# The opening of a stream encoder: five early v blocks of one column piece, a written order on every engine, x in the tiles' own rooms

## The chip, the cores and the metric

The kernel runs on one core of a Trainium2 chip. The metric is the device time of one execution in microseconds. Three runs of the kernel before took 2201.74 to 2204.34 us, median 2202.23.

## The reference

One step of a two-layer encoder for 1024 prompt frames and 32 sample frames, 1024 channels, in float32. Layer 0 mixes by a gated MLP, layer 1 by pooling; each is followed by a feed-forward part. Only the beginning of layer 0 matters here:

```python
mod = jax.nn.silu(c) @ w_ada[i] + b_ada[i]
sh1, sc1, gt1, sh2, sc2, gt2 = jnp.split(mod[:, None, :], N_MOD, axis=-1)
h = rmsnorm(x, g_norm[i, 0]) * (1 + sc1) + sh1
...
z = jax.nn.gelu(h @ w_in)
u, v = jnp.split(z, 2, axis=-1)
v = rmsnorm(v, g_v)
```

The condition c goes through SiLU and a matrix of 6144 columns to shifts and scales; x is normalised, scaled and shifted to h; the right half of h @ w_in is v, 2048 columns wide. All of v is needed before its norm, and so before the gating, can go on.

## The kernel before, in words

**Tiles.** The frames stand in three tiles of 384, 384 and 256 + 32 columns, with channels on the partitions: `acc[t]` holds x transposed. x comes in nine blocks of 128 frames (the ninth has the 32 sample frames); `do_x` squares a block on ACT for the sum of squares and transposes it with eight matmuls (line 548), and DVE copies the two halves into `acc` (line 551).

**Split products.** Every operand of a large product is split in two float32r parts: hh and hl for h, wh and wl for a weight. `do_w` makes wh on ACT (line 392) and wl on DVE (a helper at line 79) from a raw load of 512 KB. A product of a block with eight 128-row slices of a weight piece then takes 24 matmuls, three per slice (lines 876 to 878): wh with hh, wl with hh, wh with hl. `v_mm` issues them, `v_end` applies the GELU, sums squares and stores the result to `vd` (line 890).

**v in pieces and blocks.** v has four column pieces p of 512, and nine blocks b of frames (blocks 0 to 2 are tile 0, 3 to 5 tile 1, 6 to 8 tile 2). A piece's weight comes in four items q, two channel slices each.

**The ada slices.** Shifts and scales come in slices of 256 columns, each from two loads. The first eight slices (0 to 3 shift, 4 to 7 scale) are multiplied on TensorE (`do_ada_pe`, line 424: four matmuls per load, which the trace shows as eight); ACT copies the result (adas, line 436), two matmuls transpose it (adat, line 441), DVE reduces it (adar, line 443) and writes `mod` and `coef`. Later slices are summed on DVE (aa).

**The norm of a tile.** `first_norm(t)` is a generator. Its first part is `spread`: DVE makes the factor per frame (ms_h, r_h), ACT writes it on diagonals (line 684), TensorE broadcasts them (pb_h, line 686) and ACT copies the result (line 840). Then `apply` goes through the eight channel slices: mt on DVE (x times coef times factor), hh on ACT (plus shift, rounded, line 823), hl on DVE (the rest). Each `next` advances it by a slice.

**The opening.** Five blocks get PSUM banks at once: (0,0), (0,1), (0,2), (1,0), (1,1), as (piece, block), all of tile 0. In round q (0 to 3) the ada slices 4+q and q, the items q of both pieces, and two slices of tile 0's norm are made, then the five blocks take their products with item q, 30 matmuls. In between, round 2 takes x blocks 3 to 5 and tile 1's statistics, round 3 blocks 6 to 8 and tile 2's. After the rounds come the rest of the norms, the ends of the five blocks, and then the other blocks in `v_order`, first (1,2), then blocks 3 to 8 of pieces 0 and 1, then pieces 2 and 3.

**Loads.** `stream` is the list of loads in the order in which they are made into operands; `issue` puts them on SP's queue ahead of use. x, the v items and later loads take one of three raw buffers; the early ada loads take slots of the weight pool (16). The row vectors (conditions, norm gains, biases) are loaded from ACT's queue at the very beginning.

**Order.** The instructions are recorded in the order of the program, and a scheduler may move them within an engine. `time["dve"]` and `time["pe"]` are the planner's own clocks, which decide when later stream items are taken in; they measure nothing.

Of the kernel before, what the change touches and what calls it, by code (L numbers as in the profile page):

```python
# [15 lines left out]
P = 128  # L16
D = 1024
# [17 lines left out]
def tile_stream_encoder_step(  # L35
# [119 lines left out]
    def t_raw(name):  # L155
        return work.tile([P, 1024], F32, tag="raw", bufs=RAW_SLOTS, name=name)
# [9 lines left out]
            (sgu_g_v.rearrange("o (k p) -> (o k) p", p=P), 16),  # L166
        ],
    ]
    vecs = []
    for i, parts in enumerate(rows):  # L170
        n = sum(k for _, k in parts)
        raw = t_m(f"row{i}")
        at = 0
        for ap, k in parts:
            nc.scalar.dma_start(raw[at : at + k, :P], ap)
            at += k
        if i == 2:
            act(out=raw[0:16, P : 2 * P], in_=raw[0:16, :P], func=AF.Silu)
        pt = ps_ms(f"rowT{i}")
        nc.tensor.transpose(pt[:, :n], raw[:n, :P], ident[:n, :n])  # L180
        if i == 2:
            nc.tensor.transpose(pt[:, 64:80], raw[0:16, P : 2 * P], ident[0:16, 0:16])
        v = const.tile([P, n], F32, name=f"vec{i}")
        nc.vector.tensor_copy(v, pt[:, :n])
        vecs.append(v)
        if i == 2:
            csil = const.tile([P, KB, NV], F32, name="csil")
            nc.vector.tensor_copy(csil, pt[:, 64:80].rearrange("p (v k) -> p k v", v=NV))
            csil32 = work.tile([P, NV, 256], F32, tag="aa", bufs=2, name="csil32").rearrange(
                "p v (k m) -> p (v k) m", m=32  # L190
            )[:, 0:KB, :]
            nc.vector.memset(csil32, 0.0)
            nc.vector.tensor_copy(csil32[:, :, 0:NV], csil)
    gT = vecs[0]
    bT = vecs[1]
    pscale = vecs[2][:, 16:24]
# [127 lines left out]
    for b in range(3):  # L324
        add_x(b)
    for q in range(4):
        if q == 3:
            for b in range(3, 6):
                add_x(b)
        for j in (8 + 2 * q, 9 + 2 * q, 2 * q, 2 * q + 1):  # L330
            add_ada(0, j)
        for p in range(2):
            add_w(*v_item(p, q))
    first_ada = len(stream)
    for b in range(6, 9):
# [28 lines left out]
    deferred = []  # L364

    def in_raw(k):
        return not (stream[k][0] == "ada" and k < first_ada)
# [439 lines left out]
    def apply(t, l, cf, sh, r, keep=False):  # L807
        hh[t] = room("h", t, f"hh{l}_{cf}_{t}", F32R)
        hl[t] = room("l", t, f"hl{l}_{cf}_{t}", F32R)
        for k in range(KB):  # L810
            for c0, w, v in segs[t]:
                x = A(t, k, c0, w)
                a = t_m(f"mt{t}_{k}_{v}")[:, :w] if keep else x
                stt(
                    out=a,
                    in0=x,
                    scalar=coef[:, l, cf, v, k : k + 1],
                    in1=r[:, c0 : c0 + w],
                    op0=ALU.mult,
                    op1=ALU.mult,  # L820
                )
                b = mod[:, l, sh * 8 + k, v : v + 1]
                act(out=hh[t][:, k, c0 : c0 + w], in_=a, func=AF.Identity, bias=b, scale=1.0)
                stt(
                    out=hl[t][:, k, c0 : c0 + w],
                    in0=a,
                    scalar=b,
                    in1=hh[t][:, k, c0 : c0 + w].bitcast(F32),
                    op0=ALU.add,
                    op1=ALU.subtract,  # L830
                )
            yield False
# [24 lines left out]
    def v_mm(ps, p, b, ks):  # L857
        if b < 8:
            t, c0, m = min(b // 3, 2), (b - 3 * min(b // 3, 2)) * P, P
        else:  # L860
            t, c0, m = 2, 256, DEC
        for k in ks:
            wh, wl = need_w(("v", p, k // 2))
            o = (k % 2) * 512
            if b == 8:
                a = hs[k // 4][:, k % 4, :]
                tick(0.46)
                mm(ps[: 2 * m, :], a, wh[:, o : o + 512], start=k == 0, stop=False)
# [7 lines left out]
            mm(ps[:m, :], a_h, wh[:, o : o + 512], start=k == 0, stop=False)  # L876
            mm(ps[:m, :], a_h, wl[:, o : o + 512], start=False, stop=False)  # L877
            mm(ps[:m, :], a_l, wh[:, o : o + 512], start=False, stop=k == KB - 1)  # L878
# [25 lines left out]
    early_ps = [(ps_dn if i < 3 else ps_up)(f"pv{p}_{b}") for i, (p, b) in enumerate(early)]  # L904
    h0, h1, h2 = (first_norm(t) for t in range(NT))
    stream_to("x", 2)
    statistics(h0)
    stream_to("ada", (0, 0, 1))
    for q in range(4):
        stream_to("w", ("v", 0, q))  # L910
        next(h0)
        stream_to("w", ("v", 1, q))
        next(h0)
        if q < 2:
            stream_to("ada", (0, q + 1, 1))
        elif q == 2:
            stream_to("x", 5)
            statistics(h1)
            stream_to("ada", (0, 3, 1))
        else:  # L920
            stream_to("x", 8)
            statistics(h2)
        for ps, (p, b) in zip(early_ps, early):
            v_mm(ps, p, b, (2 * q, 2 * q + 1))
    for h in (h0, h1):
        for _ in h:
            pass
    for ps, (p, b) in zip(early_ps, early):
        v_end(ps, p, b)
    for _ in h2:  # L930
        pass

    hs = []
    for half in range(2):
# [619 lines left out]
```

## Time and profile before

| what | value |
|---|---|
| median of three runs | 2202.23 us |
| the profiled execution's own time | 2204.23 us |
| its span, first to last instruction | 2202.4 us |
| mean granted TensorE clock | 0.998 |
| early x blocks | 9 loads, 512 KB each but the last |
| loads of the first four rounds (x blocks 6 to 8 with them) | 33 |

The profile has a page of totals and views of the trace. A row of the timeline gives start and duration in us, engine, line, operation, what is written and read, shapes, how many instructions are merged (x16), and in brackets how long the engine had been idle and what ended that. PE is TensorE; PEld is its weight load, which runs beside it; ACT is ScalarE, DVE is VectorE, SP issues most loads; a q behind an engine's name means the issue of transfers. A window row gives start and end, length, and for each engine its busy us and number of instructions, then the granted TensorE clock, the busy share of the DMA engines, and GB/s.

### The profile page before, as it was taken

How to read it: one execution, taken by the hardware profiler on the slowest of the kernel's cores; microseconds unless marked ns; L12 is line 12 of the kernel's file. 1: busy time of each engine (PE TensorE's matmuls, PEld its weight loads, DVE VectorE, ACT ScalarE, POOL GpSimd, SP SyncE). 2: the span in 40 equal slices, each digit the busy share in tenths (PEclk: the TensorE clock that was granted, in tenths of full speed). 3: DMA queues.
4: the chain of work that ended last, by engine and by line, in shares of the span. 5: the costliest groups of instructions: out<-in, count | busy, mean ns of one | idle time of the engine just before them, and what ended most of it. 6: DMA issues, size and time to landing. Idle time of an engine off the chain costs nothing.

```text
span 2202.4 us, 33445 instructions
## 1 busy us (share of the span) xinstructions
PE 2179.8 (99%) x13383; PEld 2095.2 (95%) x13383; DVE 1378.1 (63%) x2439; ACT 986.7 (45%) x1675; POOL 0.7 (0%) x6
## 2 busy tenths in 40 slices
PE   7999999999999999999999999999999999999998
PEld 4777899999999999999999999999999999999998
DVE  4945746566869546575747879879775554523375
ACT  4633422134447552323445566656564542313354
POOL 0000000000000000000000000000000000000000
PEclk9999999999999999999999999999999999999999
DMA  8565624343527443344645465655454552302343
GB/s 278 181 210 166 198 87 131 89 144 117 154 82 220 148 147 122 101 133 122 191 126 153 149 179 177 183 184 158 142 171 143 154 153 64 109 10 77 97 121 111
DMA packets 354753, 312.98 MB, mean 142 GB/s; under 512 B 10819, under 2 KB 316427, under 8 KB 354597
## 3 DMA queue, kind: packets, MB, share of 16 engines
q1 hardware_dynamic: 352596, 309.95, 46.2%
q8 instruction: 105, 1.72, 0.3%
q10 hardware_dynamic: 2000, 0.89, 0.2%
q14 instruction: 52, 0.42, 0.1%
HBM read 278.95 MB, written 31.84 MB: 141 GB/s over the span
## 4 chain that ended last, share of the span: by engine, by line
PE 97%; DMA 1%; ACT 1%; DVE 1%; issue 0%; SPq 0%; DVEq 0%; ACTq 0%
PE pf L849 11%; PE pf L850 11%; PE pf L851 11%; PE pg L849 11%; PE pg L850 11%; PE pg L851 11%; PE pu L849 3%; PE pu L851 3%; PE pu L850 3%; PE po L849 3%; PE po L850 3%; PE po L851 3%; PE pv L876 3%; PE pv L877 2%; PE pv L878 2%; PE psp L1096 1%
## 5 line engine op out<-in xcount | busy, mean ns | idle before, releaser
L849 PE MATMUL pg<-fh,wh_dn 128*128 128x384 f32 (+1 forms) x1536 | 498.9, 325 | 0.0
L849 PE MATMUL pf<-hh,wh_up 128*128 128x384 f32 (+1 forms) x1536 | 497.0, 324 | 0.0
L850 PE MATMUL pf<-hl,wh_up 128*128 128x384 f32 (+1 forms) x1536 | 496.5, 323 | 0.0
L851 PE MATMUL pf<-hh,wl_up 128*128 128x384 f32 (+1 forms) x1536 | 495.6, 323 | 0.0
L850 PE MATMUL pg<-fl,wh_dn 128*128 128x384 f32 (+1 forms) x1536 | 494.8, 322 | 0.0
L851 PE MATMUL pg<-fh,wl_dn 128*128 128x384 f32 (+1 forms) x1536 | 493.9, 322 | 0.0
L849 PEld LDWEIGHTS pg<-fh,wh_dn 128*128 128x128 f32 x1536 | 288.5, 188 | 4.4 <-issue 3.3
L79 DVE TENSOR_TENSOR wl_up<-raw,wh_up 128x1024 fp32r<-128x1024 f32 x152 | 185.9, 1224 | 168.1 <-ACT wh_up L392 168.1
L850 PEld LDWEIGHTS pg<-fl,wh_dn 128*128 128x128 f32 x1536 | 288.6, 188 | 0.9 <-DVE fl L79 0.2
L849 PEld LDWEIGHTS pf<-hh,wh_up 128*128 128x128 f32 x1536 | 288.3, 188 | 1.3 <-issue 0.8
L851 PEld LDWEIGHTS pg<-fh,wl_dn 128*128 128x128 f32 x1536 | 288.7, 188 | 0.0
L850 PEld LDWEIGHTS pf<-hl,wh_up 128*128 128x128 f32 x1536 | 288.1, 188 | 0.4
L851 PEld LDWEIGHTS pf<-hh,wl_up 128*128 128x128 f32 x1536 | 288.2, 188 | 0.0
L392 ACT ACTIVATE wh_up<-raw 128x1024 fp32r<-128x1024 f32 x152 | 161.1, 1060 | 278.2 <-PE pf L850 215.9
L79 DVE TENSOR_TENSOR acc<-acc,pg 128x384 f32<-128x384 f32 (+1 forms) x336 | 174.1, 518 | 165.2 <-PE pg L851 164.0
L392 ACT ACTIVATE wh_dn<-raw 128x1024 fp32r<-128x1024 f32 x152 | 161.0, 1060 | 217.6 <-PE pg L850 178.6
L79 DVE TENSOR_TENSOR wl_dn<-raw,wh_dn 128x1024 fp32r<-128x1024 f32 x152 | 186.0, 1224 | 85.8 <-ACT wh_dn L392 85.5
L79 DVE SCALAR_TENSOR_TENSOR aa<-raw,csil,aa 128x512 f32<-128x512 f32 (+1 forms) x364 | 204.3, 620 | 6.0 <-DMA raw<-in_w_ada_dram 5.8
L1178 ACT ACTIVATE r<-pf 128x384 f32<-128x384 f32 (+1 forms) x192 | 86.7, 452 | 195.6 <-PE pf L851 193.0
L79 DVE TENSOR_TENSOR fl<-r,fh 128x384 fp32r<-128x384 f32 (+1 forms) x192 | 100.4, 523 | 103.6 <-ACT fh L1006 102.3
L849 PE MATMUL pu<-hh,wh_u 128*128 128x384 f32 (+1 forms) x384 | 126.8, 330 | 0.0
L849 PE MATMUL po<-ush,wh_o 128*128 128x384 f32 (+1 forms) x384 | 124.1, 323 | 0.0
(253 smaller groups left out, 2912.6 us busy)
## 6 DMA issues: line engine op xcount, KB each, us to landing
raw<-in_ffn_w_up_dram SPq DMA_DIRECT2D x152, 512.0 KB, 4.1
raw<-in_ffn_w_down_dram SPq DMA_DIRECT2D x152, 512.0 KB, 3.5
raw<-in_w_ada_dram SPq DMA_DIRECT2D x96, 512.0 KB, 4.1
raw<-in_sgu_w_in_dram SPq DMA_DIRECT2D x40, 512.0 KB, 4.6
xd<-acc SPq DMA_DIRECT2D x8, 1536.0 KB, 7.8
raw<-in_sgu_w_out_dram SPq DMA_DIRECT2D x24, 512.0 KB, 3.8
xo_r<-xd SPq DMA_DIRECT2D x32, 384.0 KB, 3.7
vd<-vt SPq DMA_DIRECT2D x32, 256.0 KB, 2.8
```

Of the source, the lines that this page charges most:

```text
L79: return op(out, *args, **kw)
L392: act(out=wh, in_=r, func=AF.Copy)
L849: mm(ps[:, :n], wh, rh, start=i == 0, stop=False)
L850: mm(ps[:, :n], wh, rl, start=False, stop=False)
L851: mm(ps[:, :n], wl, rh, start=False, stop=i == last)
L876: mm(ps[:m, :], a_h, wh[:, o : o + 512], start=k == 0, stop=False)
L877: mm(ps[:m, :], a_h, wl[:, o : o + 512], start=False, stop=False)
L878: mm(ps[:m, :], a_l, wh[:, o : o + 512], start=False, stop=k == KB - 1)
L1096: mm(sp[:, c * P : (c + 1) * P], vl[:, c, k * P : (k + 1) * P], wr[:, c * P : (c + 1) * P], start=True, stop=True,)
L1178: act(out=r[:, :n], in_=ps[:, :n], func=AF.Relu)
```

## The change

The row vectors are loaded and turned by three functions in place of one loop: the conditions come first, are activated and transposed by themselves (`turn_conditions`), and the other rows are transposed later (`turn_vectors`), between x blocks 1 and 2.

The x loads go to the room of their tile's hh (`x_rows`), which is free until then; only block 8 takes a raw buffer. Block 2's load is issued from ACT's queue. In the stream, blocks 3 to 5 stand right behind round 0's loads, items of piece 1 behind the four rounds.

The early blocks are (0,0) to (0,4), of which 0 to 2 are tile 0 and 3 and 4 tile 1. A round makes tile 0's slices, takes item q of piece 0 and multiplies blocks 0 to 2; then tile 1's slices, the ada slices of the next round, and blocks 3 and 4. Tile 1's statistics stand in round 0, behind the products of blocks 0 to 2. All of it stands in `tc.manual_schedule()`: each engine runs its instructions in the order in which the program lists them. Behind the rounds follow block 5's 24 products, the four items of piece 1, and tile 2's statistics and norm.

`apply` with `keep` takes slices in pairs for tiles of one segment: two mt, two hh, two hl. `v_order` starts with piece 1's blocks 0 to 5, then blocks 6 to 8 of both pieces. The planner's DVE clock is set 12 ahead of TensorE's behind the opening, not 4.

```diff
+    def turn_conditions():
+        raw = vec_rows[2]
+        nc.vector.memset(csil32, 0.0)
+        act(out=raw[0:16, P : 2 * P], in_=raw[0:16, :P], func=AF.Silu)
+        pt = ps_ms("csilT")
+        nc.tensor.transpose(pt[:, 0:16], raw[0:16, P : 2 * P], ident[0:16, 0:16])
...
+    def turn_vectors():
+        for raw, v in zip(vec_rows, vecs):
+            n = v.shape[1]
+            pt = ps_ms("rowT")
+            nc.tensor.transpose(pt[:, :n], raw[:n, :P], ident[:n, :n])
+            nc.vector.tensor_copy(v, pt[:, :n])
...
     for q in range(4):
-        if q == 3:
+        for j in (8 + 2 * q, 9 + 2 * q, 2 * q, 2 * q + 1):
+            add_ada(0, j)
+        add_w(*v_item(0, q))
+        if q == 0:
             for b in range(3, 6):
                 add_x(b)
-        for j in (8 + 2 * q, 9 + 2 * q, 2 * q, 2 * q + 1):
-            add_ada(0, j)
-        for p in range(2):
-            add_w(*v_item(p, q))
     first_ada = len(stream)
-    for b in range(6, 9):
-        add_x(b)
+    add_x(6)
+    add_x(7)
+    for q in range(4):
+        add_w(*v_item(1, q))
+        if q == 1:
+            add_x(8)
...
+            elif kind == "x":
+                r = x_rows[key // 3][:, key % 3, :]
...
-                i = nc.sync.dma_start(r[:nr, :], ap)
+                i = (nc.scalar if key == 2 else nc.sync).dma_start(r[:nr, :], ap)
...
-        for k in range(KB):
-            for c0, w, v in segs[t]:
+        parts = [[(k, *seg) for seg in segs[t]] for k in range(KB)]
+        if keep and len(segs[t]) == 1:
+            parts = [parts[k] + parts[k + 1] for k in range(0, KB, 2)]
...
-    early = [(0, 0), (0, 1), (0, 2), (1, 0), (1, 1)]
...
+    early_ps = [(ps_dn if b < 3 else ps_up)(f"pv0_{b}") for b in range(5)]
...
+    with tc.manual_schedule():
+        load_vectors(2, slice(0, 2))
+        issue()
+        load_vectors(2, slice(2, 4))
+        load_vectors(0, slice(0, 1))
+        load_vectors(1, slice(0, 1))
+        turn_conditions()
+        stream_to("x", 1)
+        turn_vectors()
+        stream_to("x", 2)
+        stream_to("ada", (0, 4, 1))
+        statistics(h0)
+        stream_to("ada", (0, 0, 1))
+        for q in range(4):
+            next(h0)
+            stream_to("w", ("v", 0, q))
+            early_mm((0, 1, 2), q)
+            if q == 0:
+                stream_to("x", 5)
+                statistics(h1)
+            next(h1)
+            if q < 3:
+                stream_to("ada", (0, q + 1, 1))
+            else:
+                early_end((0, 1, 2))
+            early_mm((3, 4), q)
+        early_end((3, 4))
+        stream_to("x", 7)
+        ps = ps_dn("pv0_5")
+        v_mm(ps, 0, 5, range(KB))
+        stream_to("w", ("v", 1, 3))
+        v_end(ps, 0, 5)
+        statistics(h2)
...
-    v_order = [(1, 2)]
-    v_order += [(p, b) for p in range(2) for b in range(3, 9)]
+    v_order = [(1, b) for b in range(6)] + [(p, b) for p in range(2) for b in range(6, 9)]
     v_order += [(p, b) for p in range(2, 4) for b in range(9)]
-    time["dve"] = time["pe"] + 4.0
+    time["dve"] = time["pe"] + 12.0
```

More of the change, by code (lines that the diff above doesn't have):

```diff
@@ L168, in tile_stream_encoder_step @@
     ]
[L169 to L175, printed above, removed]
-            at += k
[L177 to L193, printed above, removed]
+    vec_rows = [t_m(f"row{i}") for i in range(3)]
@@ new lines, in tile_stream_encoder_step, with load_vectors @@
+    vecs = [
+        const.tile([P, sum(k for _, k in parts)], F32, name=f"vec{i}")
+        for i, parts in enumerate(rows)
+    ]
+    def load_vectors(i, part):
+        at = sum(k for _, k in rows[i][: part.start])
+        for ap, k in rows[i][part]:
+            nc.scalar.dma_start(vec_rows[i][at : at + k, :P], ap)
+            at += k
+    csil = const.tile([P, KB, NV], F32, name="csil")
+    csil32 = work.tile([P, NV, 256], F32, tag="aa", bufs=2, name="csil32").rearrange(
+        "p v (k m) -> p (v k) m", m=32
+    )[:, 0:KB, :]
@@ L366, in in_raw @@
     def in_raw(k):
-        return not (stream[k][0] == "ada" and k < first_ada)
+        kind, key = stream[k][:2]
+        return key == 8 if kind == "x" else not (kind == "ada" and k < first_ada)
+    x_rows = [
+        room("h", t, f"x_rows{t}")
+        .rearrange("p k n -> p (k n)")[:, : ncol[t] // P * D]
+        .rearrange("p (b d) -> p b d", d=D)
+        for t in range(NT)
+    ]
     def issue():
@@ L809, in apply @@
         hl[t] = room("l", t, f"hl{l}_{cf}_{t}", F32R)
-        for k in range(KB):
-            for c0, w, v in segs[t]:
+        parts = [[(k, *seg) for seg in segs[t]] for k in range(KB)]
+        if keep and len(segs[t]) == 1:
+            parts = [parts[k] + parts[k + 1] for k in range(0, KB, 2)]
+        for part in parts:
+            xs = []
+            for k, c0, w, v in part:
                 x = A(t, k, c0, w)
@@ L821, in apply @@
                 )
+                xs.append(a)
+            for a, (k, c0, w, v) in zip(xs, part):
                 b = mod[:, l, sh * 8 + k, v : v + 1]
                 act(out=hh[t][:, k, c0 : c0 + w], in_=a, func=AF.Identity, bias=b, scale=1.0)
+            for a, (k, c0, w, v) in zip(xs, part):
                 stt(
@@ L826, in apply @@
                     in0=a,
-                    scalar=b,
+                    scalar=mod[:, l, sh * 8 + k, v : v + 1],
                     in1=hh[t][:, k, c0 : c0 + w].bitcast(F32),
@@ L900, in stream_to, with early_mm, early_end @@
         run_deferred()
-    early = [(0, 0), (0, 1), (0, 2), (1, 0), (1, 1)]
-    early_ps = [(ps_dn if i < 3 else ps_up)(f"pv{p}_{b}") for i, (p, b) in enumerate(early)]
+    early_ps = [(ps_dn if b < 3 else ps_up)(f"pv0_{b}") for b in range(5)]
     h0, h1, h2 = (first_norm(t) for t in range(NT))
[L906 to L926, printed above, removed]
-            pass
[L928 to L931, printed above, removed]
+    def early_mm(bs, q):
+        for b in bs:
+            v_mm(early_ps[b], 0, b, (2 * q, 2 * q + 1))
+    def early_end(bs):
+        for b in bs:
+            v_end(early_ps[b], 0, b)
+    with tc.manual_schedule():
[31 more added lines that the diff above has]
+        statistics(h2)
+        for _ in h2:
+            pass
     hs = []
```

2 lines of the change are left out of this document (added).

## The prediction

> **What bounds the kernel now.** I read the page's totals and chain first, then the busy windows of the opening, then the opening instruction by instruction.
>
> ```profile
> span 2202.4 us, 33445 instructions
> PE 2179.8 (99%) x13383; PEld 2095.2 (95%) x13383; DVE 1378.1 (63%) x2439; ACT 986.7 (45%) x1675; POOL 0.7 (0%) x6
> PE 97%; DMA 1%; ACT 1%; DVE 1%; issue 0%; SPq 0%; DVEq 0%; ACTq 0%
> ...
> 0.00:24.70 24.70, 13.38 (x86) 8.43 (x86) 9.11 (x50) 11.54 (x20) 0.70 (x6) 0.93 0.91 301
> 24.70:76.00 51.30, 48.24 (x283) 34.06 (x284) 34.81 (x81) 29.95 (x53) 0.00 (x0) 0.97 0.71 234
> 76.00:144.20 68.20, 68.20 (x320) 52.43 (x320) 52.20 (x138) 31.48 (x74) 0.00 (x0) 1.00 0.72 238
> 24.70:76.00 51.30, 34.99 (x131) 23.62 (x132) 0.00 (x0) 1.91 (x4) 0.97 0.71 234
> 76.00:144.20 68.20, 67.06 (x287) 51.66 (x287) 0.67 (x1) 19.98 (x47) 1.00 0.72 238
> ...
> 77.05 0.39 PE L876 MATMUL pv<-wh_v,hh 128*128 128x512 f32 x1
> 77.28 0.39 PE L877 MATMUL pv<-wl_v,hh 128*128 128x512 f32 x1
> ```
>
> TensorE sets the end: 97% of the chain. So the change is worth exactly what it does to TensorE's idle time before the products run without a break. The window rows (span, then PE, PEld, DVE, ACT, POOL, granted clock, DMA share, GB/s; the last two rows hold the v products alone) put that moment at 76 us. From there to 144.2 us, where the first two column pieces end, TensorE is full: 287 products, 0.23 us apart by the two timeline rows. Before it, 51.3 us hold only 131 products, 30.1 us of work. "Busy" in those windows hides this, because a matmul's row (0.39) is longer than its spacing (0.23).
>
> **The yardstick.** Both kernels must reach the end of piece 1, then run the same list. I take the time at which each has issued 144 v products, and correct for what else is done by then. Before: 131 at 76 us, 13 more at 0.23 make 79.0 us, and there all nine x blocks and all three norms' broadcasts are done.
>
> **What the change removes and moves.** Five early blocks of two pieces become five of piece 0 (three of tile 0, two of tile 1), so the early rounds need four v items, not eight. x goes to the tiles' own rooms: blocks 3 to 5 are loaded ahead of round 1, and no longer wait for three raw buffers; block 2 is issued from ACT's queue. Every engine's order is fixed as written. The loads before the last early round shrink from 33 to 26 (9 x, 16 ada, 8 v against 6, 16, 4), at 0.524 MB each.
>
> ```profile
> 27.50:30.00 2.50, 2.50 (x15) 1.97 (x12) 1.03 (x5) 1.13 (x3) 0.00 (x0) 1.00 1.03 343
> 30.00:32.50 2.50, 1.11 (x5) 0.56 (x3) 2.19 (x3) 1.32 (x2) 0.00 (x0) 1.00 1.07 364
> 32.50:35.00 2.50, 1.09 (x16) 0.39 (x16) 0.08 (x1) 0.00 (x0) 0.00 (x0) 0.92 1.11 345
> 35.00:37.50 2.50, 2.50 (x16) 1.14 (x12) 0.26 (x2) 1.76 (x3) 0.00 (x0) 0.50 0.54 188
> ...
> 33.13 0.64 PE L424 MATMUL ada<-raw,csil 128*32 128x256 f32 x8 [2.02 <-DMA raw<-in_w_ada_dram]
> 34.55 1.08 PE L424 MATMUL ada<-raw,csil 128*32 128x256 f32 x8 [0.78 <-DMA raw<-in_w_ada_dram]
> ```
>
> At 343 to 364 GB/s a load takes 1.5 us. These windows are a stall on loads of before, and the change removes it: in steady state a round needs five loads, 7.5 to 8 us, and the 26th load is there near 42 us (the first at 4.6, 25 more at 1.5). I find the new rounds longer than 8 us, so the loads stop being the bound. The saving is real but it uncovers the norm's chain.
>
> **The new opening, step by step.** Rows of before give each duration and hand-over:
>
> ```profile
> 0.74 3.82 DMA raw<-in_x_prompt_dram
> 1.32 0.59 ACTq L175 DMA_DIRECT2D row<-in_b_ada_dram  x1
> 7.72 1.28 ACT L178 ACT_TABLE_LOAD   x1
> 9.01 0.31 ACT L178 ACTIVATE row<-row 16x128 f32<-16x128 f32 x1
> 9.69 0.20 DVE L184 COPY vec<-rowT 128x40 f32<-128x40 f32 x1 [2.70 <-PE rowT L182]
> 9.59 5.15 PE L548 MATMUL xT<-ident,raw 128*128 128x128 f32 x24
> 21.59 1.07 PE L424 MATMUL ada<-raw,csil 128*32 128x256 f32 x16
> 22.40 1.15 DVE L79 SCALAR_TENSOR_TENSOR mt<-acc,coef,r_h 128x384 f32<-128x384 f32 x2
> 22.73 0.38 ACT L436 ACTIVATE adas<-ada 128x256 f32<-128x256 f32 x1 [1.56 <-PE ada L424]
> 23.01 1.05 ACT L392 ACTIVATE wh_v<-raw 128x1024 fp32r<-128x1024 f32 x1
> 23.16 0.44 PE L441 MATMUL adat<-ident,adas 128*128 128x128 f32 x2 [0.50 <-ACT adas L436]
> 23.64 0.17 DVE L443 TENSOR_REDUCE adar<-adat 128x4 f32<-128x16 f32 x1
> 24.05 1.12 ACT L823 ACTIVATE hh<-mt,mod 128x384 fp32r<-128x384 f32 x2
> 24.09 1.23 DVE L79 TENSOR_TENSOR wl_v<-raw,wh_v 128x1024 fp32r<-128x1024 f32 x1
> 24.71 0.97 PE L876 MATMUL pv<-wh_v,hh 128*128 128x512 f32 x3
> 48.38 2.04 PE L548 MATMUL xT<-ident,raw 128*128 128x128 f32 x16
> 49.02 2.49 DVE L551 COPY acc<-xT 128x512 f32<-128x512 f32 x4 [2.65 <-PE xT L548]
> 53.04 0.16 DVE L79 TENSOR_SCALAR ms_h<-ssx 128x3 f32<-128x3 f32 x1
> 54.27 0.99 ACT L684 ACTIVATE r_h<-ident,r_h 128x128 f32<-128x128 f32 x3 [0.83 <-DVE r_h L79]
> 55.98 0.49 PE L686 MATMUL pb_h<-r_h,ones 128*128 128x128 f32 x2
> 56.51 0.49 ACT L840 ACTIVATE r_h<-pb_h 128x384 f32<-128x384 f32 x1 [1.25 <-PE pb_h L686]
> ```
>
> *First product.* On ACT the b_ada load now waits for x block 0 (4.6 us), and the Silu stands behind it: 0.6 issue, 1.28 table, 0.31 make 6.8 us. Then x is transposed; DVE's six copies (0.62 each) and five small ones (0.2) end near 12.8. The first ada slice costs 2.05 from matmul to reduce (21.59 to 23.64) and 0.65 for mod and coef: 15.4. Statistics: 1.23 to the diagonals, 0.99, 0.55 for the broadcast matmuls, 0.5 for the copy: 18.6. The second slice runs from 18.0 and gives its shift at 20.4. Then one mt (0.6), two hh (1.12), wh (1.05): first product 23.3, against 24.71. wl ends at 24.5; 17 products later, 28.4 us, tile 0 has done round 0. Bounds: 20 us if the transposes and copies overlap fully, 26 us if block 2 comes late.
>
> *Tile 1's statistics.* In TensorE's fixed order the transposes of blocks 3 to 5 stand behind those 18 products although the blocks landed long before. From 28.4: 0.64 to the first copy, six copies 3.73, then 1.23, 0.99, 0.55, 0.5: tile 1's factor is there at 36.1. ACT's fixed order puts both hh of tile 1 ahead of the ada copy, so the copy comes at 38.0 (0.6 for each mt, then hh 0.57); transposes, second slice (2.05) and mod end at 41.3; mt, hh, wh, wl (0.6, 1.12, 1.05, 1.23, with gaps) at 45.4; 17 products at 49.3. Between 28.4 and 49.3 TensorE has 30 products (6.9), 24 transposes (2.9) and about 3.6 of ada and broadcasts: some 7.5 us idle.
>
> *Rounds 2 and 3* repeat one chain. From the first ada matmul: 1.14 to the copy, 0.43 to the transposes, 0.37 to the second slice, 2.05 to its reduce, 0.4 to mt, 0.6, 1.12, 1.05, 1.25 for wl, 17 x 0.23: 12.4 us. TensorE's own work in it is 30 products, two slices and four transposes, 9.7 us. So round 3 of tile 0 ends at 49.3 + 24.8 = 74.1; tile 1's twelve products 76.9; transposes of blocks 6 and 7 (16, 0.12 each) 78.8; the 24 products of block 5 84.3; block 8's eight transposes 85.0.
>
> *Sum.* 144 products at 85.0 us, against 79.0, and the third tile's broadcast (six matmuls, 0.8) is still owed: +6.8. What follows adds 0 to 3: v items 2 and 3 of piece 1 wait on SP behind the stores of the early blocks and for raw buffers freed by wl (0.5), and the third tile's norm, 32 mt and hl at no more than 0.58 each (18.6 us) with ada sums between them, has from 85 to 118 us (six blocks of 5.5). Half-rate stretches, priced below, add 0 to 6. I take +1 for these together: +8. Pairing in apply costs nothing, since before already ran two mt, two hh; the separate csil transposes replace one for one; 12 instead of 4 in the planner's DVE time moves ada sums later within a stretch where DVE is busy 52 of 68 us, and from the third column piece TensorE's list is unchanged.
>
> The profiled execution took 2204.23 us, the runs' median is 2202.23; I add the difference to the median: **2210 us**.
>
> **Clock.** The row at 35.00 shows a granted clock of 0.50 right after the thin windows at 30 to 35. The Trainium skill ("TensorE: Matmul & The Clock Gate", "What's actually happening") says an idle window of about 3.4 us halves the clock and about 3.4 us of busy time restores it. By it the new order, idle before 23 us and again before 40, would begin bursts at half rate; an estimate from that page, 1.7 us for the first of them, makes the sum +8.5 instead of +6.8. The trace agrees at 35.00 for one burst.
>
> The Trainium skill ("DMA: Bandwidth & Descriptors", "Issuing engines are not separate DMA queues") says transfers begun by different engines share the same 16 DMA engines, which save only issue time. By it block 2 from ACT's queue gains nothing but its place, which the walk assumes; no run here shows it yet.
>
> **Rivals.** (A) *Not slower: rounds at the pace of loads.* If mt, hh and the split of the next round slip under the current round's products, a round takes 8 us instead of 12.4, at three rounds -13: 2197 us. For: DVE has only some 7 us of work in a round, ACT 4. Against: the products of tile 0 need the ada slice issued directly after the previous ones. It decides below 10.1 us per round (no loss) and gives a gain over 0.2% below 8.6. (B) *Same: the walk is too dear by 4 to 7 us*, the opening being at its 20 us bound or tile 1's factor three us sooner: 2204 us. For: before's transposes there ran slowly, 5.15 us for 24. Against: the three-buffer copies on DVE are 3.7 us however fast they come. (C) *Slower still: half rate.* Each gap followed by 3 us of work at half rate costs 1.5 us; four gaps add 6 to the 6.8: 2215 us. For: the 0.50 row, 2.5 us long, which cost some 1.25. Against: idle gaps inside the later rounds are 0.5 to 1.3 us each, shorter than the stall at 30 to 35. That the change does not act is no case: the loads and orders do move.
>
> **Numbers.** Forecast 0.60 (2205 to 2213), A 0.12, B 0.16, C 0.12. About 0.2%, 4.4 us, is what a measurement can tell from none. Faster: most of A, 0.11. Same: B, A's rest, and the forecast's lowest end, 0.22. Slower: 0.67. The range 2201 to 2217 leaves out most of A and C's tail.
>
> **What would show it.** Right: first product near 23 us; tile 1's transposes directly behind 18 products; three rounds about 12.4 us apart, no TensorE wait on ada loads; block 5's products ending near 84; from there TensorE full. Wrong: rounds of 8 to 10 us, block 5 ending before 78, or a wait on loads still standing in the rounds.

## The result and the profile after

The changed kernel takes 2219.25 us (median of four runs, 2217.71 to 2219.73), the kernel before beside it 2202.58 (2201.74 to 2204.34): ratio 1.0073, 95% interval 1.0056 to 1.0091. The sign of the forecast holds, its size does not: 2210 was said, with 2217 as the upper end. The profiled execution took 2219.73 us.

Page of the changed kernel (totals, then the shares of the chain that ended last), and the windows of its v products alone (start and end, length, TensorE busy us and number, granted clock, share of the DMA engines, GB/s):

```profile
span 2217.9 us, 33431 instructions
PE 2184.8 (99%) x13383; PEld 2098.4 (95%) x13383; DVE 1379.1 (62%) x2439; ACT 986.5 (44%) x1674; POOL 0.7 (0%) x6
PE 95%; DMA 2%; ACT 1%; SPq 1%; DVE 1%; issue 0%; ACTq 0%; DVEq 0%
```

```profile
24.70:76.00 51.30, 27.12 (x95) 0.85 0.47 159
76.00:144.20 68.20, 62.52 (x261) 1.00 0.47 156
```

The work is the same, 13383 matmuls, and still TensorE's: the span grew by 15.5 us because TensorE has fewer v products behind it at each moment. At 76 us it has done 95, before 131; from there to 144.2 it does 261, before 287. The granted clock over the opening fell from 0.97 to 0.85, and the DMA engines' share from 0.71 to 0.47: in the rounds the loads now wait for the kernel, not the kernel for the loads.

TensorE's timeline of the opening:

```profile
24.21 0.79 PE L905 MATMUL pv<-wh_v,hh 128*128 128x512 f32 x1 [3.27 <-ACT wh_v L414]
...
26.49 0.63 PE L905 MATMUL pv<-wh_v,hh 128*128 128x512 f32 x1
26.92 0.63 PE L906 MATMUL pv<-wl_v,hh 128*128 128x512 f32 x1
...
30.20 0.39 PE L905 MATMUL pv<-wh_v,hh 128*128 128x512 f32 x1
30.43 0.39 PE L906 MATMUL pv<-wl_v,hh 128*128 128x512 f32 x1
...
31.58 3.23 PE L570 MATMUL xT<-ident,x_rows 128*128 128x128 f32 x24
37.49 1.65 PE L708 MATMUL pb_h<-r_h,ones 128*128 128x128 f32 x6 [2.68 <-ACT r_h L706]
39.08 1.94 PE L446 MATMUL ada<-raw,csil 128*32 128x256 f32 x16
54.07 1.07 PE L446 MATMUL ada<-raw,csil 128*32 128x256 f32 x16
66.57 1.07 PE L446 MATMUL ada<-raw,csil 128*32 128x256 f32 x16
89.29 0.68 PE L570 MATMUL xT<-ident,raw 32*128 32x32 f32 x8
```

Read it against the forecast's walk. The first product starts at 24.21 (23.3 said). Then rows 0.43 us apart (26.49 to 26.92) and, from 30.2, 0.23 apart: the first eleven of the 18 products and part of the twelfth ran at half rate. Tile 1's transposes stand directly behind them, at 31.58 (28.4 said), its broadcast at 37.49, and the ada slice of round 2 begins at 54.07 (49.3). The same slice takes 1.94 us at 39.08 and 1.07 at 54.07. The next one follows at 66.57, 12.5 us later (12.4 said), and block 8's transposes come at 89.29 (84.3). So the opening ends 5.0 us later than the walk, and 4.8 of them are lost before round 2.

The second loss stands behind block 5, on TensorE, ACT and SP:

```profile
89.90 1.11 SPq L406 DMA_DIRECT2D raw<-in_sgu_w_in_dram  x2
93.65 1.06 ACT L414 ACTIVATE wh_v<-raw 128x1024 fp32r<-128x1024 f32 x1 [3.06 <-DMA raw<-in_sgu_w_in_dram]
94.76 0.50 PE L905 MATMUL pv<-wh_v,hh 128*128 128x512 f32 x1 [0.90 <-ACT wh_v L414]
96.98 1.06 ACT L414 ACTIVATE wh_v<-raw 128x1024 fp32r<-128x1024 f32 x1 [2.27 <-DMA raw<-in_sgu_w_in_dram]
98.09 0.73 PE L905 MATMUL pv<-wh_v,hh 128*128 128x512 f32 x2 [0.52 <-ACT wh_v L414]
99.35 0.51 PE L906 MATMUL pv<-wl_v,hh 128*128 128x512 f32 x1 [0.53 <-DVE wl_v L79]
```

Items 2 and 3 of piece 1 are issued from 89.90, when the wl of items 0 and 1 has freed their raw buffers. ACT can begin on them at 93.65 and 96.98, some 4 and 7 us later, and TensorE waits for each. In the profiled execution 14 products take the 5.9 us from 93.5 to 99.35, where 14 x 0.23 = 3.2 would do: 2.7 us lost.

### The profile page after: what moved, and what is told of

The parts are those of the page before. It is cut to its first block, busy times and chain, and to the rows that moved or that the text cites. A ratio compares the mean times of both kernels' runs of the same rounds, so it can differ in the third digit from the quotient of the medians.

```text
span 2217.9 us, 33431 instructions
## 1 busy us (share of the span) xinstructions
PE 2184.8 (99%) x13383; PEld 2098.4 (95%) x13383; DVE 1379.1 (62%) x2439; ACT 986.5 (44%) x1674; POOL 0.7 (0%) x6
## 4 chain that ended last, share of the span: by engine, by line
PE 95%; DMA 2%; ACT 1%; SPq 1%; DVE 1%; issue 0%; ACTq 0%; DVEq 0%
PE pf L878 11%; PE pf L880 11%; PE pg L878 11%; PE pg L880 11%; PE pg L879 11%; PE pf L879 11%; PE pu L878 3%; PE pu L880 3%; PE po L878 3%; PE po L879 3%; PE po L880 3%; PE pu L879 3%; PE pv L906 2%; PE pv L905 2%; PE pv L907 2%; PE psp L1143 1%
## 5 line engine op out<-in xcount | busy, mean ns | idle before, releaser
L878 PE MATMUL pf<-hh,wh_up 128*128 128x384 f32 (+1 forms) x1536 | 502.7, 327 | 0.0
L879 PE MATMUL pf<-hl,wh_up 128*128 128x384 f32 (+1 forms) x1536 | 490.5, 319 | 0.0
```

Source lines behind the costliest of these rows:

```text
L878: mm(ps[:, :n], wh, rh, start=i == 0, stop=False)
L879: mm(ps[:, :n], wh, rl, start=False, stop=False)
```

## The experiments

Every kernel was timed beside the kernel before on the same chip; the differences are between those medians, the intervals those of the ratio. Over the five chips the kernel before had medians of 2202.3 to 2204.8 us.

| kernel | median us (range) | over before | ratio, 95% |
|---|---|---|---|
| the change | 2219.25 (2217.71 to 2219.73) | 16.7 | 1.0056 to 1.0091 |
| the change again | 2219.62 (2216.50 to 2222.75) | 17.3 | 1.0066 to 1.0100 |
| scheduler's order | 2213.24 (2212.11 to 2219.01) | 10.4 | 1.0030 to 1.0078 |
| extra matmuls, three places | 2217.33 (2213.79 to 2218.94) | 14.5 | 1.0039 to 1.0085 |
| items of piece 1 in the rounds | 2218.83 (2217.08 to 2219.21) | 16.0 | 1.0047 to 1.0092 |
| next ada slices ahead | 2213.18 (2211.67 to 2214.16) | 10.3 | 1.0025 to 1.0071 |
| tile 1's transposes ahead | 2213.80 (2212.86 to 2215.66) | 9.9 | 1.0028 to 1.0062 |
| ada ahead, items in rounds | 2212.77 (2212.58 to 2214.23) | 8.9 | 1.0024 to 1.0054 |
| two pieces, scheduler | 2207.19 (2205.36 to 2208.97) | 3.3 | 1.0005 to 1.0024 |
| two pieces, scheduler, 12 | 2207.13 (2205.24 to 2208.57) | 2.3 | 1.0000 to 1.0019 |
| two pieces, fixed order | 2219.23 (2217.85 to 2220.39) | 15.4 | 1.0051 to 1.0081 |
| before, with the rooms | 2205.91 (2204.36 to 2207.02) | 1.1 | 0.9993 to 1.0012 |
| extras, two places, 16 and 22 | 2219.97 (2219.46 to 2223.40) | 15.2 | 1.0057 to 1.0087 |
| items ahead of the ends | 2221.96 (2221.26 to 2223.90) | 17.1 | 1.0064 to 1.0094 |
| extras, two places, 30 and 22 | 2220.46 (2218.73 to 2222.62) | 18.2 | 1.0068 to 1.0098 |
| x8 behind item 2 | 2218.25 (2215.14 to 2221.92) | 16.0 | 1.0058 to 1.0088 |

### Which part of the change costs it

**The scheduler's order for the changed program.**

```diff
-    with tc.manual_schedule():
+    with ExitStack():
```

> The changed kernel with its opening left to the scheduler, as before; loads, rooms, early blocks and pairs stay. Theory (the loss is waiting in a fixed order): the scheduler puts tile 1's transposes and the ada slices of round 1 ahead of the first products, so block 5 ends some 6 to 10 us earlier than 89.2 us and the time falls from 2219 to 2209 to 2213. Rival (one column piece gives TensorE too little work for any order): 2217 to 2220, and block 5 ends near 89 us again.

10.4 us over before, not 16.7, at the upper edge of what the theory said, though one of its runs took 2219.01 and the two intervals overlap. Its TensorE timeline:

```profile
26.72 3.93 PE L570 MATMUL xT<-ident,x_rows 128*128 128x128 f32 x24
...
43.72 2.23 PE L905 MATMUL pv<-wh_v,hh 128*128 128x512 f32 x5
```

The scheduler puts tile 1's transposes ahead of every product, starts the products only at 43.72, 19 us after the changed kernel, and is still not slower: by then both tiles' factors exist, and from there to 110 us TensorE has no wait at all. An early first product is worth little here.

**Two pieces again, with everything else of the change** (rooms, block 2 on ACT's queue, the vectors' functions, pairs), by the scheduler, and in the fixed order:

```diff
         add_w(*v_item(0, q))
+        add_w(*v_item(1, q))
...
-    early_ps = [(ps_dn if b < 3 else ps_up)(f"pv0_{b}") for b in range(5)]
+    early = [(0, 0), (0, 1), (0, 2), (1, 0), (1, 1)]
+    early_ps = [(ps_dn if i < 3 else ps_up)(f"pv{p}_{b}") for i, (p, b) in enumerate(early)]
...
+        stream_to("w", ("v", 1, q))
+        if q == 0:
+            stream_to("x", 5)
...
-    time["dve"] = time["pe"] + 12.0
+    time["dve"] = time["pe"] + 4.0
```

> The loads, the rooms, block 2 on ACT's queue, the vectors' functions and the pairs of the change, but before's five blocks of two pieces, all of tile 0, before's v order and the scheduler's order. Theory (the loss is that blocks of one piece give a tile's chain only 18 products to hide behind, not 30, and need two tiles' norms): the stall on loads of before at 30 to 35 is gone, rounds at the pace of seven loads, TensorE full from 70 to 75 us, time 2196 to 2202. Rival (the loss is in the rooms, the vectors or the pairs): 2206 or more.

> The same with every engine in the order of the program up to the third tile's statistics. Theory (a fixed order costs what it cost the changed kernel, 2219.3 against 2213.2 by the scheduler): 4 to 8 us more than the kernel by the scheduler. Rival (with 30 products behind each of tile 0's slices there is little to reorder): within 2 us of it, so that the fixed order alone is no loss.

3.3 us over before by the scheduler: the gain expected of the rooms isn't there, but most of the change's loss is gone. The fixed order adds 12 us to it, more than the 4 to 8 expected. TensorE in the fixed one:

```profile
28.81 2.82 PE L568 MATMUL xT<-ident,x_rows 128*128 128x128 f32 x12 [4.98 <-DVE acc L571]
```

Tile 1's transposes stand ahead of the first products there and wait 5 us for VectorE's copies, and the first product comes at 36.07; the third tile's broadcast waits 2.9 us, and behind it nine products run at half rate. This listing was written for the scheduler, so the 12 us are the price of this order and not of fixed orders in general.

Of the four kernels, then, one piece costs some 7 us more than two where the scheduler orders (10.4 against 3.3, on two chips), and the written order 6 and 12 us more than the scheduler's. No run takes the 7 us apart.

**The planner's 12** in the kernel of two pieces by the scheduler:

```diff
-    time["dve"] = time["pe"] + 4.0
+    time["dve"] = time["pe"] + 12.0
```

> The kernel of rooms with before's five blocks of two pieces, by the scheduler (2207.2), with the planner's DVE clock 12 ahead as in the change, not 4. There TensorE had waited 1.7 us for wr near 367 us, which neither before nor the changed kernel shows. Theory (the wait is the planner's): gone, 2205 to 2206, the same as before within 0.2%. Rival (it is the opening that is later): 2207.

The wait for wr is gone from the trace (no such row among TensorE's waits), but the median is the same 2207: over before 2.3 against 3.3. The wait had not been what the time is made of.

**The rooms alone, in the kernel before:**

```diff
-        if q == 3:
-            for b in range(3, 6):
-                add_x(b)
...
+        if q == 1:
+            for b in range(3, 6):
+                add_x(b)
...
+            elif kind == "x":
+                r = x_rows[key // 3][:, key % 3, :]
...
-            stream_to("x", 5)
             statistics(h1)
...
+        if q == 1:
+            stream_to("x", 5)
```

> The kernel before with one part of the change alone: x in the tiles' rooms, blocks 3 to 5 loaded behind round 1's items and transposed at its end, so that they wait for no raw buffer. Theory (the stall on loads at 30.7 to 35.6 us is what the rooms remove, about 2.8 us of TensorE's waits): 2199 to 2202, faster than before. Rival (the loads' rate sets the pace of the rounds there, the stall only moves to another load): 2203 to 2206.

The same as before (0.9993 to 1.0012). TensorE's waits (who, for whom, us in total, times, longest):

```profile
PE xT L558 <- DMA x_rows<-in_x_prompt_dram: 1.8, 3, 1.4
PE ada L434 <- DMA raw<-in_w_ada_dram: 1.6, 3, 0.8
```

The stall on ada loads of 2.8 us at 30 to 35 shrank to 1.6, and x's loads are waited for instead, 1.8. From 30 to 40 us the DMA engines' share is 1.05 to 1.07 there, as in the stall of before. So the rate of the loads seems to set that opening: taking the raw buffers away moved the wait and saved nothing. No version here beats the kernel before.

### Tile 1's transposes

**The next round's ada slices ahead of the products**, which moves x blocks 3 to 5 ahead too, because they stand before those slices in the stream:

```diff
+            if q < 3:
+                stream_to("ada", (0, q + 1, 1))
             early_mm((0, 1, 2), q)
...
-            if q < 3:
-                stream_to("ada", (0, q + 1, 1))
-            else:
+            if q == 3:
                 early_end((0, 1, 2))
```

> In each round the next round's two ada slices stand ahead of the products of blocks 0 to 2, not behind them; nothing else changes. Theory (a round is a chain from the ada slice to wl, 12.5 us against 9.7 us of TensorE work): the next round's mt, hh, wh and wl run under the products, rounds take 10 to 11 us, block 5 ends 5 us earlier, time 2213 to 2215. Rival (TensorE's own in-order waits on the ada copies set the round): rounds stay at 12 us, time 2218 to 2220.

**Only the transposes ahead:**

```diff
+            if q == 0:
+                stream_to("x", 5)
             early_mm((0, 1, 2), q)
             if q == 0:
-                stream_to("x", 5)
                 statistics(h1)
```

> Only tile 1's 24 transposes (x blocks 3 to 5) move, ahead of tile 0's first 18 products. Splits the 6 us that the kernel with the next round's slices ahead of the products gained (there the transposes moved too). Theory (the transposes in TensorE's fixed order were late, behind products): tile 1's factor comes earlier, so the second ada slice does too, but the first product comes later by what the 24 transposes and six copies take; rounds 1 to 3 stay 12.5 us apart, block 5's products end 0 to 3 us earlier, time 2216 to 2219. Rival (the gain was the transposes'): block 5 ends near 83, time 2213 to 2214.

10.3 and 9.9 us over before: the second edit alone has all the gain of the first, and the theory written for it (2216 to 2219) fell to its rival (2213 to 2214). Its interval lies wholly below that of the change's second set of runs and overlaps that of the first a little. TensorE's timeline of it:

```profile
20.82 1.47 PE L570 MATMUL xT<-ident,x_rows 128*128 128x128 f32 x12
...
28.32 0.78 PE L905 MATMUL pv<-wh_v,hh 128*128 128x512 f32 x1
...
33.37 0.83 PE L708 MATMUL pb_h<-r_h,ones 128*128 128x128 f32 x6
34.12 1.07 PE L446 MATMUL ada<-raw,csil 128*32 128x256 f32 x16
...
47.77 1.07 PE L446 MATMUL ada<-raw,csil 128*32 128x256 f32 x16
...
60.29 1.07 PE L446 MATMUL ada<-raw,csil 128*32 128x256 f32 x16
```

The first product is 4.1 us later than in the changed kernel (28.32 against 24.21), the slices of rounds 1, 2 and 3 are 5.0, 6.3 and 6.3 us earlier. TensorE begins the transposes at 20.82, in time in which it would wait, so tile 1's broadcast comes at 33.37, not 37.49: 4.1 us. The other 2.2 are half rate that went with it: from that broadcast to the slice of round 2 14.4 us, not 16.6, and the slice at 34.12 takes 1.07, not 1.94. With the ada slices ahead as well, rounds shrink to 10.9 us, but the first product comes at 35.08, and the time stays:

```profile
46.64 1.07 PE L446 MATMUL ada<-raw,csil 128*32 128x256 f32 x16
...
57.51 1.07 PE L446 MATMUL ada<-raw,csil 128*32 128x256 f32 x16
```

### The half rate

**Extra matmuls** (128 x 128, overwritten by the real ones) keep TensorE busy where it waits: 18 ahead of tile 0's broadcast, 28 ahead of the first products, 24 ahead of tile 1's broadcast; later only at the last two places, with 16 and 22, and with 30 and 22.

```diff
+    warm = {"h0_0": 18, "h0_1": 24}
...
         pb = ps_ms(f"pb_{tag}")
+        for _ in range(warm.get(tag, 0)):
+            mm(pb[:, :P], onesr, onesr, start=True, stop=True)
...
             stream_to("w", ("v", 0, q))
+            if q == 0:
+                for _ in range(28):
+                    mm(early_ps[0][:, :P], onesr, onesr, start=True, stop=True)
             early_mm((0, 1, 2), q)
```

> 18, 28 and 24 extra matmuls whose results are overwritten stand in TensorE's three longest gaps (before tile 0's broadcast, before the first products, before tile 1's broadcast). Theory (half rate costs 4.8 us between 16 and 48 us): the granted clock stays at 1.0 from 25 to 47 us, round 1 of tile 0 ends near 50 instead of 54.1 us, time 2214 to 2216. Rival (waits alone, the clock is hidden by them): 2219 or, since the extra matmuls take time, 2220 to 2221.

> The changed kernel with overwritten 128x128 matmuls in two places where TensorE only waits: 16 behind the first second ada slice (ahead of the first products), 22 behind tile 1's transposes (ahead of its broadcast). None ahead of tile 0's broadcast, where 18 of them had put the start back by 3.3 us. Theory (half rate is 4 to 5 us of the loss and lies on the chain): first product at 24 to 25 as in the changed kernel, its 18 products 0.23 apart, the ada slice of round 2 by 49.5 to 51 instead of 54.07, time 2215 to 2216. Rival (the half rate only fills time in which TensorE would wait for the vector engines): 2218 or more.

> Overwritten 128x128 matmuls in the same two places as before, but 30 instead of 16 ahead of the first products, so that TensorE is busy until these begin; 22 ahead of tile 1's broadcast. Theory (half rate is 4 to 5 us of the loss, on the chain; 16 were too few because TensorE fell idle again for 1.5 us): the 18 first products 0.23 apart, from first product to the ada slice of round 2 some 25 to 26 us instead of 29.9, time 2 to 5 us below the changed kernel on the same chip. Rival (those products' rate is hidden by the chain behind them): within 1 us of it.

The first (three places), on TensorE:

```profile
16.16 4.08 PE L708 MATMUL pb_h<-ones 128*128 128x128 f32 x18
20.04 1.59 PE L712 MATMUL pb_h<-r_h,ones 128*128 128x128 f32 x6
...
27.54 0.51 PE L909 MATMUL pv<-wh_v,hh 128*128 128x512 f32 x1 [0.19 <-ACT wh_v L414]
...
53.41 1.07 PE L446 MATMUL ada<-raw,csil 128*32 128x256 f32 x16
```

From the first product to the slice of round 2 it needs 53.41 - 27.54 = 25.9 us; the changed kernel 54.07 - 24.21 = 29.9. So 4.0 us of half rate lay on the chain between them in that execution. The time gained only 2.2 of that and lies between theory and rival, and the first product came 3.3 us later. The next run, which has no extras ahead of the broadcast, also starts late, at 26.48, so that only 1.1 of the 3.3 are theirs, less than its expectation took for granted.

With 16 and 22, windows of TensorE, then its timeline:

```profile
22.50:25.00 2.50, 2.18 (x18) 1.00 1.10 351
25.00:27.50 2.50, 0.79 (x1) 0.61 1.09 365
27.50:30.00 2.50, 2.26 (x5) 0.50 1.07 350
```

```profile
22.97 1.98 PE L967 MATMUL pv<-ones 128*128 128x128 f32 x16
26.48 0.79 PE L909 MATMUL pv<-wh_v,hh 128*128 128x512 f32 x1 [1.53 <-ACT wh_v L414]
...
39.80 1.07 PE L712 MATMUL pb_h<-r_h,ones 128*128 128x128 f32 x6
...
54.42 1.07 PE L446 MATMUL ada<-raw,csil 128*32 128x256 f32 x16
```

The 16 extras had the clock back at 1.00 in 22.5 to 25, but they end 1.5 us before the first product, and the products run at half rate all the same. The second place works: from tile 1's broadcast to the slice of round 2 14.6 us, where the changed kernel needs 16.6 (37.49 to 54.07). The time, 2219.97, is the rival's all the same; in the profiled execution the first ada slice ran at half rate, so that the start was late, and TensorE waits 2.4 us far behind the opening (0.6 for wr, 1.8 near the end), which the change does not. With 30 extras the first place works too:

```profile
26.24 0.50 PE L909 MATMUL pv<-wh_v,hh 128*128 128x512 f32 x1
...
52.34 1.07 PE L446 MATMUL ada<-raw,csil 128*32 128x256 f32 x16
```

26.1 us from first product to round 2. Still its time is 18.2 us over before, no less than the change's: the rival's number. Three things took the gain back in the profiled execution. The first product came at 26.24, 2 us late, because the first ada slice, ahead of any extra, ran at half rate here. Items 2 and 3 cost it 1.6 us (two gaps between 94.28 and 96.53). And far behind the opening TensorE waits 1.1 us for wr, an operand that VectorE makes, which it does in neither profile of the change:

```profile
PE psp L1150 <- DVE wr L79: 1.1, 1, 1.1
```

Such a wait for wr, 0.5 to 1.7 us, stands in six of the kernels here (next ada slices ahead, transposes ahead, two pieces by the scheduler, items ahead of the ends, and both runs of two places), so a difference of 1 us between medians says little of the opening. So the trace places the half rate on the chain, three times over, but the run with the cleanest cure did not get faster, and the times do not confirm the 4 us by themselves.

**The change once more**, on the chip of that run:

> The changed kernel as it is, on the chip of the next two, so that each is compared with it and not across chips. Every theory: 15 to 18 us more than the kernel before. If the first ada slice runs at half rate (x16 in 1.94 us, not 1.07), as in some profiles, the first product comes at 26.4, not 24.2, and the time is 2 to 4 us above the other runs.

```profile
24.27 0.80 PE L905 MATMUL pv<-wh_v,hh 128*128 128x512 f32 x1 [3.26 <-ACT wh_v L414]
...
52.66 1.07 PE L446 MATMUL ada<-raw,csil 128*32 128x256 f32 x16
...
92.95 0.50 PE L905 MATMUL pv<-wh_v,hh 128*128 128x512 f32 x1 [0.44 <-ACT wh_v L414]
```

28.4 us where the first profile had 29.9, and one short gap behind block 5, worth 0.6 us, where there had been three: span 2214.7 against 2217.9. The two losses are not constants; they differ by 1.5 and 2.1 us between two executions of one kernel. So the cure of the half rate is worth 2.3 us against this execution and 4 against the first. On this chip the account of the run with 30 extras closes: 2.0 us later start, 2.3 less to round 2, 1.0 more for the items and the 1.1 for wr make 1.8 of the 2.2 us by which its span is longer. Whether the same two losses spread the change's four runs over 6 us is not shown: only one of them has a trace, and nineteen runs of the kernel before on another chip spread over 6.7.

### The late v items

**Items 0 and 1 of piece 1 split behind rounds 1 and 2; behind rounds 2 and 3 with the ada slices ahead; and behind round 3 ahead of the ends:**

```diff
+    add_w(*v_item(1, 0))
+    add_w(*v_item(1, 1))
     add_x(6)
     add_x(7)
...
             early_mm((3, 4), q)
+            if q in (1, 2):
+                stream_to("w", ("v", 1, q - 1))
```

```diff
             early_mm((3, 4), q)
+            if q == 2:
+                stream_to("w", ("v", 1, 0))
...
+            if q == 3:
+                stream_to("w", ("v", 1, 1))
                 early_end((0, 1, 2))
```

```diff
+        stream_to("w", ("v", 1, 1))
         early_end((3, 4))
```

> Items 0 and 1 of piece 1 are loaded ahead of x blocks 6 and 7 and split behind rounds 1 and 2, where ACT and DVE idle; raw buffers come free 20 us earlier. Theory (items 2 and 3 of piece 1 cost 2.7 us of gaps at 93 to 99 us by waiting for raw buffers): the gaps go, time 2216 to 2217. Rival (the gaps are the price of the third tile's x and move elsewhere): 2219.

> The next round's ada slices ahead of the products (as in the run that took 2213.2), and items 0 and 1 of piece 1 loaded behind round 3's item and split behind rounds 2 and 3. Theory (TensorE's gaps at 93 to 99 came from late raw buffers, and the split has room in the last rounds once these no longer wait for ada): 2.0 to 2.7 us less than that run, 2210.5 to 2211.5. Rival (ACT and DVE in a fixed order wait for the items, as when they were split behind rounds 1 and 2): the gap moves into round 3, 2213 or more.

> The changed kernel with items 0 and 1 of piece 1 first behind the rounds in the stream, and split right behind blocks 3 and 4's last products, ahead of their ends, so that their raw buffers come free about 10 us sooner. Theory (2.7 us of the loss are TensorE's gaps between 93 and 99.4, by the late loads of items 2 and 3): no gap behind block 5, 2.0 to 2.7 us less, 2216.5 to 2217.5. Rival (ACT, nearly full from 75 to 90, puts the ends of the early blocks or block 5's start later by the two splits): 2218.5 or more.

The first, on ACT and TensorE:

```profile
67.15 1.15 ACT L852 ACTIVATE hh<-mt,mod 128x384 fp32r<-128x384 f32 x2 [2.01 <-DVE mt L79]
67.82 0.61 PE L906 MATMUL pv<-wh_v,hh 128*128 128x512 f32 x1 [4.08 <-ACT hh L852]
```

Behind block 5 TensorE has no gap any more, but the edit moved more than it meant to. The stream is taken in order, so behind round 1 it brings round 3's ada slices and items 2 and 3 of piece 0 along with item 0 of piece 1. VectorE makes two wl (2.36 us from 64.22) ahead of round 2's mt, hh comes behind that, and TensorE waits 4.08 us for round 2's first product; the nine products behind the wait run at half rate. The gap moved, and the time is 16.0 over before, as the rival said. The third is no faster either (17.1): the transposes of block 7 wait 2.5 us, since DVE's copies stand behind the two wl. The second, where rounds no longer wait for ada, has no wait for wh or wl behind block 5 and is 1.4 us nearer to before than the same kernel without the splits (8.9 against 10.3, on two chips), within what the intervals leave open.

**x block 8 behind item 2**, so that the third raw buffer goes to item 2 at once:

```diff
-        if q == 1:
+        if q == 2:
             add_x(8)
```

> The changed kernel with x block 8, which takes a raw buffer, behind item 2 of piece 1 in the stream, not ahead of it. Theory (TensorE's gaps at 93 to 99 are the late loads of items 2 and 3, because x8 holds the third raw buffer): item 2 is loaded with items 0 and 1, only item 3 waits, half or more of the 2.7 us goes, time 1 to 2.5 us below the changed kernel on the same chip. Rival (wh and wl of the items, in ACT's and DVE's fixed order, are late anyway): within 0.7 us of it.

```profile
86.29 2.94 ACT L414 ACTIVATE wh_v<-raw 128x1024 fp32r<-128x1024 f32 x3
88.65 0.50 PE L906 MATMUL pv<-wl_v,hh 128*128 128x512 f32 x1 [0.24 <-DVE wl_v L79]
```

Three wh in a row, and 0.24 us is all that TensorE waits between 84 and 100 us. So x8 did hold the buffer that item 2 needed. What that costs is less clear: with x8 in its place the same chip's execution of the change waited only 0.44 us (item 3 could be used 5 us after its issue there, not 7), and the two spans are alike (2214.8 and 2214.7). The time, 1.4 us under the change on the same chip, is inside the spread of both.

## Why the prediction was right or wrong

**The walk at full clock: right.** Its 26.0 us from first product (23.3) to round 2 (49.3) is 25.9 and 26.1 in the two runs that kept TensorE warm there; rounds are 12.5 (12.4 said). No round waits for an ada load, so the stall on loads did give way to the norm's chain. Rival A (rounds of 8 us) is out. Rival B too: neither the opening's 20 us bound nor an earlier tile 1 appeared.

**Tile 1's statistics: right, and the heart of the loss.** The forecast had the transposes behind 18 products at 28.4 and called TensorE idle for 7.5 us up to 49.3. Moving only them brought the slice of round 2 6.3 us forward: 4.1 by the earlier broadcast, which is most of the +6.8 of the sum, and 2.2 by half rate that went with it.

**The failed step is "Half-rate stretches, priced below, add 0 to 6. I take +1 for these together".** The forecast knew the price (1.5 us for a gap) and had counted four gaps, then left them to a rival with 0.12. Measured in the profiled execution, against the walk's own steps: 0.9 up to the first product (the second ada slice took 1.87 us there, not 1.07), 2.3 in round 0's products (24.21 to 31.58 is 7.4, said was 5.1), 0.7 back at tile 1's copies, 2.3 from its broadcast to round 2 (16.6 against 14.3 at full rate): 4.8. In the other profiled execution of the change the same account gives 3.4 (round 2 at 52.66). They belonged into the likeliest case: each stands on a chain that the walk itself had found unbroken, behind a gap that it had worked out.

**The second mis-sized term is v items 2 and 3 of piece 1, "(0.5)"**: 2.7 us in that execution, 0.6 in the other. The place was named; x8 as holder of the third buffer wasn't.

**Sum:** 6.8, + 5.0 for the later opening, + 2.7 late items = 14.5 of the 15.5 us by which the span grew; 1.0 stays unplaced. The other execution gives 6.8 + 3.6 (block 8's transposes at 87.93) + 0.6 = 11.0 of 12.3. The third tile's norm cost nothing, as said: behind 99.35 TensorE's waits have no row for it.

**Rival C had the mechanism and about its size** (6 for 5). Its 2215 lacks what every case lacked, the late items' 2.7 and the 1.0: with these it would be 2218.7. That the sizes lie so near is in part luck: it had four gaps at 1.5 us, and the trace has three stretches of 0.8 to 2.3. The range's upper end, 2217, was 2.3 us short of the median.

The Trainium skill ("TensorE: Matmul & The Clock Gate", "What's actually happening") has half rate after an idle window of about 3.4 us. Here 1.53 us of idle time behind 2 us of dense matmuls were enough (the row at 26.48), so that figure is no safe bound for gaps. In the kernel before, too, the matmuls at 34.55 began at half rate behind waits of 2.02 and 0.78 us with full-rate matmuls between them. By that page the forecast had an estimate of 1.7 us for one burst; two bursts cost 2.3 us each in the first execution, 1.4 and 1.7 in the other.

## What to carry to other kernels

When an order is fixed by hand, list for each engine which instructions are ready long before their turn, and what their results gate: here 24 transposes, 3.2 us of work on data that had landed, stood behind 18 products and cost 4 us, and 2 more by half rate, while the early product that they made room for was worth nothing. Where a walk finds TensorE idle for 2 to 4 us ahead of a chain, put the matmuls behind it into the sum at half rate, not into a rival. A wait for buffers that is taken away at one place is only gone if what is brought forward doesn't stand ahead of something urgent in another engine's order; in three of five attempts here it moved (the rooms in the kernel before, the items in the rounds, the items ahead of the ends).

## What the runs showed of the hardware

The clock's phase is not the kernel's. Up to the first ada slice, the kernels in the fixed order that differ only later issue the same instructions, yet the slice's 16 matmuls took 1.07 us in some profiles and 1.94 in others, and the first product, where nothing was put ahead of it, came 2 us later (26.4 against 24.2). Of the change, run again:

```profile
12.49 1.07 PE L446 MATMUL ada<-raw,csil 128*32 128x256 f32 x16
```

and of the run with 30 and 22 extras:

```profile
13.46 1.94 PE L446 MATMUL ada<-raw,csil 128*32 128x256 f32 x16
```

Five of eleven such profiles had the first, six the second. The Trainium skill ("TensorE: Matmul & The Clock Gate", "What's actually happening") says that the gate's window doesn't start with the kernel and that cold matmuls vary from run to run; these rows agree. The granted clock doesn't show it. The run with ada ahead and items in the rounds has this slice in its timeline, and this window (all engines, the clock third from the end):

```profile
13.50 1.94 PE L447 MATMUL ada<-raw,csil 128*32 128x256 f32 x16
```

```profile
10.00:15.00 5.00, 4.86 (x30) 2.86 (x28) 3.00 (x7) 0.00 (x0) 0.00 (x0) 1.00 1.01 296
```

Full rate is recorded where the matmuls run at half.
